# Gate and up as seven products of sums of quarters, and the whole modulation on TensorE

## The chip, the cores and the metric

The kernel runs on one core of one Trainium2 chip. The metric is the device time of one execution in microseconds. The kernel before takes 1740.79 us (median of 3 runs, 1739.17 to 1743.87).

## The reference

One step of a hybrid backbone on 640 token rows (512 latent tokens and 128 context tokens) of width 1024, two layers deep. Everything is float32.

```python
def trunk_layer(x, mod, s0, prm, l, pool_seg):
    sh1, sc1, g1, sh2, sc2, g2 = jnp.split(mod, N_MOD, axis=-1)
    h = rmsnorm(x, prm['norm1_g'][l]) * (1 + sc1) + sh1
    cols = jnp.einsum('bnd,de->bne', h, prm['w_in'][l])          # 1024 -> 2832 columns
    ...                                       # delta rule, spatial gating, pooling -> ya, yb, yc
    mix = jnp.einsum('bne,ed->bnd', jnp.concatenate([ya, yb, yc], axis=-1), prm['w_out'][l])
    x = x + g1 * mix
    h = rmsnorm(x, prm['norm2_g'][l]) * (1 + sc2) + sh2
    gate, up = jnp.split(jnp.einsum('bnd,df->bnf', h, prm['w_gu'][l]), 2, axis=-1)   # FF = 2816 each
    x = x + g2 * jnp.einsum('bnf,fd->bnd', jax.nn.silu(gate) * up, prm['w_down'][l])
    return x, s_fin
# mod = silu(c) @ w_mod[l] + b_mod[l]: 6 x 1024 numbers for each of two conditionings (latent, context)
```

## The kernel before, in words

Activations lie transposed: a tile holds 128 features on its rows and the 640 tokens as columns, in two halves of 320. Every large product is made three times to keep float32's accuracy: the weight block and the activations are each split into a rounded part and a rest (`wh`, `wl` and `xhi`, `xlo`, or `ah`, `al`), and `mm3` (L335) issues wh x hi, wh x lo and wl x hi as three matmuls of 128 x 128 weights on 320 columns. A weight block comes by a DMA on SyncE's queue (`wload`, L297) into one of two buffers; `wsplit` (L306) rounds it on ScalarE (L322) and takes the rest on VectorE (all but three of its 128-column blocks) and on GpSimd (the last three, L326).

A layer has three stages, and with the two layers they stand in this order: mix0, out0, ffn0, mix1, out1, ffn1.

- mix: the products with `w_in` (`gemm_xs`, L348), 22 blocks and the logits; the delta rule in chunks, and the two other branches. Many small matmuls and many steps on VectorE and ScalarE run among the large ones.
- out: the products with `w_out` (L1296), eight output blocks of 48 matmuls, each followed by the residual (`resid`, L448) and by the scaled and split operands of the next stage (`Norm.add`, L403).
- ffn: 22 units of 128 hidden columns. Each unit is two calls of `gemm_xs` (gate and up, 48 matmuls each: 8 blocks of k, 2 halves, 3 products). The norm isn't applied beforehand: the operand is x times (1 + scale), the shift rides along as two columns in front of the first half (322 columns), and each evacuation multiplies by the row statistics `rst` and adds the shift's part. After 8, 8 and 6 units the products with `w_down` follow (L1399). The last six units of layer 1 end the kernel with transposes, the final norm and the outputs.

The modulation needs 12,288 numbers per conditioning. Two sixths of layer 0 come first, as matmuls with 32 columns of weights, four row blocks side by side on four column strips of the array (`first_mod_`, L499). The other ten sixths are 160 steps of 512 columns x 128 rows (`pump_`, L257): VectorE multiplies and adds for one conditioning (L125), ScalarE multiplies for the other (L150) and GpSimd adds (L282); after eight steps `mod_sums` (L224) sums over the rows, by transposes on TensorE or by VectorE's own transpose and small matmuls. A table says how many steps follow each half of a product; they run from mix0 to the end of ffn0.

The program's instructions are ordered by a scheduler: each has a priority by its place in the program, moved by the offsets of `PRI` (L39), and each engine then takes its own in that order. PSUM has three buffers `acc`, three `dl` and two `md`.

Of the kernel before, what the change touches and what calls it, by code (L numbers as in the profile page):

```python
# [16 lines left out]
D = 1024  # L17
# [14 lines left out]
POUT = 1  # L32
# steps of the modulation after each half of a product, by branch
PUMPS = {'log0': (0, 0), 'k00': (0, 0), 'q00': (1, 2), 'sgu0': (1, 1), 'z0': (0, 1), 'v10': (1, 1), 'q10': (0, 0), 'v00': (1, 0), 'k10': (0, 1), 'pool0': (1, 0)}
# [11 lines left out]
def host_constants():  # L46
# [10 lines left out]
    # from here on: not kept on chip as they are  # L57
# [34 lines left out]
def tile_hybrid_step(ctx: ExitStack, tc: tile.TileContext,  # L92
# [59 lines left out]
    class at:  # L152
        """the instructions inside come that much earlier in the order of issue"""
# [11 lines left out]
    def behind(ins, prev):  # L165
        """queues one instruction of an engine behind another"""
# [10 lines left out]
    def in_turn(key, ins):  # L177
        """instructions of one kind in the order of the program"""
# [29 lines left out]
    quarters = const.tile([P, 32], F32, name="quarters")  # L208
    selr = const.tile([P, 15, P], F32R, name="selr")
# [9 lines left out]
    # steps: 512 columns x 128 rows of w_mod; a step's load is issued some steps ahead of its arithmetic  # L219
    SIXTHS = [(0, 2), (0, 4), (0, 3), (0, 5), (1, 1), (1, 0), (1, 2), (1, 4), (1, 3), (1, 5)]  # L220
    steps = [(l, w * D + c0, k) for l, w in SIXTHS for c0 in (0, 512) for k in range(KT)]
    ps_ = {"i": 0, "j": 0, "ma": None, "wm": {}, "due": None, "at": "mix0"}

    def mod_sums(l, c0, ma):  # L224
        t0 = c0 // P
        if ps_["at"] != "ffn0":
            for s in range(2):
                pt = md()
                for cb in range(4):
                    nc.tensor.transpose(pt[:, cb * P:(cb + 1) * P], ma[:, s, cb * P:(cb + 1) * P], ident)  # L230
                m = mod[:, l, s, t0:t0 + 4]
                nc.vector.tensor_reduce(m, pt.rearrange("p (c n) -> p c n", c=4), op=ADD, axis=AX.X)
                tt(m, m, bmod[:, l, t0:t0 + 4], ADD)
            mod_scales(l, c0)
            return
        # sums over the 32 rows of each quarter, then over the quarters
        ms = sm.tile([P, 2, 16], F32, tag="ms", name="ms", bufs=1)
        for s in range(2):
            pt = md()
            nc.vector.transpose(pt, ma[:, s])  # L240
            nc.vector.tensor_reduce(ms[:, s], pt.rearrange("p (c n) -> p c n", n=32), op=ADD, axis=AX.X)
        pt = md()
# [1194 lines left out]
```

## Time and profile before

| | |
|---|---|
| runs | 1740.79 us median, 1739.17 to 1743.87 |
| span of the profiled execution | 1737.7 us |
| PE busy | 1666.4 us (96%), 12952 matmuls |
| DVE, ACT, POOL busy | 1155.2 (66%), 761.1 (44%), 585.3 us (34%) |
| chain that ended last | PE 53%, of which the large products (`acc`) 47% |
| DMA | 174.34 MB, mean 100 GB/s |

The span is what the profile shows of one execution; the shortest run lies 1.5 us above it, the median 3.1 us. PE's mean duration of a matmul (316 ns) isn't its price: matmuls are pipelined, and from start to start there is less. A stretch's price is read from how many matmuls start in it. Idle time of an engine other than PE costs nothing unless PE waits for it.

### The profile page before, as it was taken

How to read it: one execution, taken by the hardware profiler on the slowest of the kernel's cores; microseconds unless marked ns; L12 is line 12 of the kernel's file. 1: busy time of each engine (PE TensorE's matmuls, PEld its weight loads, DVE VectorE, ACT ScalarE, POOL GpSimd, SP SyncE). 2: the span in 40 equal slices, each digit the busy share in tenths (PEclk: the TensorE clock that was granted, in tenths of full speed). 3: DMA queues.
4: the chain of work that ended last, by engine and by line, in shares of the span. 5: the costliest groups of instructions: out<-in, count | busy, mean ns of one | idle time of the engine just before them, and what ended most of it. 6: DMA issues, size and time to landing. Idle time of an engine off the chain costs nothing.

```text
span 1737.7 us, 33153 instructions
## 1 busy us (share of the span) xinstructions
PE 1666.4 (96%) x12952; PEld 1603.2 (92%) x12952; DVE 1155.2 (66%) x2462; ACT 761.1 (44%) x1564; POOL 585.3 (34%) x578
## 2 busy tenths in 40 slices
PE   6999999998899999999999999999999999999997
PEld 4788989988899999999998899999999999999997
DVE  6698688799888688877467777675544434433454
ACT  4557765554444344434246656543322212321232
POOL 3342330367645454554164112013411221222110
PEclk8999999999999999999999999999999999999999
DMA  9431231444444544453241211113222222222221
GB/s 316 143 98 57 68 99 29 150 127 139 145 141 141 154 137 143 143 158 103 62 144 52 62 38 50 37 51 126 83 73 74 79 79 74 74 73 73 74 85 61
DMA packets 243379, 174.34 MB, mean 100 GB/s; under 512 B 10006, under 2 KB 212376, under 8 KB 243224
## 3 DMA queue, kind: packets, MB, share of 16 engines
q1 hardware_dynamic: 231888, 157.44, 29.8%
q10 hardware_dynamic: 10184, 12.29, 2.2%
q0 software_dynamic: 1152, 2.51, 0.4%
q8 instruction: 102, 1.67, 0.4%
q14 instruction: 53, 0.43, 0.1%
HBM read 163.29 MB, written 8.91 MB: 99 GB/s over the span
## 4 chain that ended last, share of the span: by engine, by line
PE 53%; DVE 3%; ACT 1%; issue 1%; POOL 0%; DMA 0%; DVEq 0%; POOLq 0%; ACTq 0%
PE acc L117 47%; PE dl L117 5%; DVE wl L122 0%; PE md L117 0%; DMA w<-in_w_down_dram 0%; PE dl L1379 0%; DVE cv L125 0%; POOL guh L830 0%; PE md L760 0%; DVE yt L125 0%; DVE st L125 0%; DVE Z L122 0%; ACT wh L322 0%; ACT MT L945 0%; DVE SI L122 0%
## 5 line engine op out<-in xcount | busy, mean ns | idle before, releaser
L117 PE MATMUL acc<-xhi,wh 128*128 128x322 f32 (+2 forms) x2112 | 667.4, 316 | 5.4 <-DVE ga L122 4.6
L117 PE MATMUL acc<-xlo,wh 128*128 128x322 f32 (+2 forms) x2112 | 666.0, 316 | 1.4 <-DVE xlo L125 1.2
L117 PE MATMUL acc<-xhi,wl 128*128 128x320 f32 (+1 forms) x2080 | 655.0, 315 | 5.1 <-DVE wl L122 5.1
L326 POOL TENSOR_TENSOR wl<-w,wh 128x384 fp32r<-128x384 f32 x188 | 258.7, 1376 | 792.5 <-ACT wh L322 777.9
L117 PEld LDWEIGHTS acc<-xhi,wh 128*128 128x128 f32 (+1 forms) x2112 | 399.4, 189 | 10.7 <-PE acc L117 7.2
L117 PEld LDWEIGHTS acc<-xlo,wh 128*128 128x128 f32 (+1 forms) x2112 | 400.2, 189 | 4.1 <-POOL spp L1148 1.5
L117 PEld LDWEIGHTS acc<-xhi,wl 128*128 128x128 f32 x2080 | 396.4, 191 | 6.6 <-DVE wl L122 5.9
L322 ACT CAST wh<-w 128x1024 fp32r<-128x1024 f32 (+1 forms) x188 | 194.5, 1035 | 343.4 <-PE acc L117 282.6
L282 POOL TENSOR_TENSOR ma<-ma,wm 128x512 f32<-128x512 f32 x140 | 207.2, 1480 | 133.5 <-ACT wm L150 113.8
L122 DVE TENSOR_TENSOR wl<-w,wh 128x640 fp32r<-128x640 f32 (+1 forms) x188 | 213.3, 1134 | 50.5 <-ACT wh L322 23.9
L117 PE MATMUL acc<-ah,wh 128*128 128x320 f32 (+2 forms) x632 | 195.6, 309 | 0.7 <-ACT ah L1322 0.7
L117 PE MATMUL acc<-al,wh 128*128 128x320 f32 (+2 forms) x632 | 195.1, 309 | 0.1
L117 PE MATMUL acc<-ah,wl 128*128 128x320 f32 (+2 forms) x632 | 195.1, 309 | 0.0
L150 ACT ACTIVATE wm<-wm,sc 128x512 f32<-128x512 f32 x140 | 101.1, 723 | 135.0 <-DVE ma L125 117.8
L125 DVE SCALAR_TENSOR_TENSOR x<-acc,mod,x 128x128 f32<-128x128 f32 (+3 forms) x192 | 77.9, 434 | 119.8 <-PE acc L117 119.5
L125 DVE SCALAR_TENSOR_TENSOR ma<-wm,sc,ma 128x512 f32<-128x512 f32 x140 | 134.9, 964 | 25.6 <-DMA wm<-in_w_mod_dram 24.7
L117 PEld LDWEIGHTS acc<-ah,wh 128*128 128x128 f32 x632 | 118.7, 188 | 1.2 <-ACT ah L1322 1.1
L117 PEld LDWEIGHTS acc<-al,wh 128*128 128x128 f32 x632 | 118.7, 188 | 0.3 <-DVE al L122 0.3
L117 PEld LDWEIGHTS acc<-ah,wl 128*128 128x128 f32 x632 | 118.7, 188 | 0.0
L1322 ACT CAST ah<-ga 128x320 fp32r<-128x320 f32 x88 | 40.5, 460 | 155.9 <-DVE ga L125 155.9
L150 ACT ACTIVATE ga<-ga,bt 128x320 f32<-128x320 f32 x132 | 57.4, 468 | 89.9 <-DVE ga L122 89.9
L122 DVE TENSOR_TENSOR ga<-acc,rst 128x320 f32<-128x320 f32 x88 | 42.4, 483 | 73.9 <-PE acc L117 73.4
(369 smaller groups left out, 2481.7 us busy)
## 6 DMA issues: line engine op xcount, KB each, us to landing
w<-in_w_gu_dram SPq DMA_DIRECT2D x88, 512.0 KB, 3.7
wm<-in_w_mod_dram SPq DMA_DIRECT2D x162, 256.0 KB, 2.9
w<-in_w_in_dram SPq DMA_DIRECT2D x44, 512.0 KB, 3.6
w<-in_w_down_dram SPq DMA_DIRECT2D x32, 512.0 KB, 4.2
w<-in_w_out_dram SPq DMA_DIRECT2D x32, 256.0 KB, 3.0
wf<-in_w_mod_dram SPq DMA_DIRECT2D x30, 256.0 KB, 6.5
w<-in_w_down_dram SPq DMA_DIRECT2D x16, 384.0 KB, 3.4
x<-xd ACTq DMA_DIRECT2D x16, 320.0 KB, 4.7
```

Source lines behind the costliest of these rows:

```text
L117: return nc.tensor.matmul(o, lhsT=l, rhs=r, start=st, stop=sp, **kw).ins
L122: recent["v"] = nc.vector.tensor_tensor(o, a, b, op=op).ins
L125: recent["v"] = nc.vector.scalar_tensor_tensor(o, a, s, b, op0=op0, op1=op1).ins
L150: recent["a"] = nc.scalar.activation(o, i, f, **kw).ins
L282: nc.gpsimd.tensor_tensor(ma[:, 1], ma[:, 1], wm, op=ADD)
L322: nc.scalar.copy(wh, v)
L326: nc.gpsimd.tensor_tensor(wl[:, c:], v[:, c:], wh[:, c:], op=SUB)
L1322: nc.scalar.copy(hi[:, sl], ga[:, sl])
```

## The change

Four parts.

1. All but the first units of ffn (4 in layer 0, 3 in layer 1, made as before, gate and up together) are made by seven products in place of eight. With the k blocks and the tokens in halves, gate and up of one unit are a product of 2 x 2 quarters. `t_sums` makes four sums and differences of the quarters of h once per layer; each unit makes sums S1 to S4 of quarters of its weights and splits them as it splits weights (`Unit.prep`). A product is 4 blocks of k x 3 = 12 matmuls of 320 columns, so a unit has 84 in place of 96. Three intermediate sums are read out of one PSUM tile between the products that add into it (`Unit.go`: P6, P7 and P4 wait for the reading before them). `NEED` and the loop at the end say in which order a unit's products and the next unit's stand.
2. So that token quarters can be added, h is normalised, scaled and shifted before the products (`stats`, then h, hhi, hlo), in two parts of 384 and 256 tokens; there are no shift columns and no `rst` in ffn's evacuations any more. The last two blocks of out are reordered so that the first part of all blocks is done first.
3. The modulation's ten sixths are 40 groups of four matmuls side by side (32 x 512), a copy of 512 columns to SBUF and four matmuls with two columns. They stand in the mix stages alone, 0.6 groups after each half of a product in layer 0 and 0.45 in layer 1.
4. The pieces of ffn are 4, 4, 4, 5, 5 units instead of 8, 8, 6, and the products with `w_down` follow each. The selection matrices `selr` are made anew in each layer.

The diff's core (comments are also removed throughout):

```diff
+SHARE = (0.6, 0.45)
-W32, WM, WHL = 2, 3, 2
+W32, WM, WHL = 2, 4, 2
+PIECES, NPL = (4, 4, 4, 5, 5), (4, 3)
+NACT, NFT, NS = 5, 5, 3
+NEED = {"P2": ("g",), "P1": (), "P5": ("S1",), "P6": ("S2",), "P7": ("S3",), "P4": ("u2",), "P3": ("S4",)}
...
+    def mod_columns(ws, l, c0, k0, msb):
+        pm = md()
+        for i, w in enumerate(ws):
+            g = 32 * (i % 4)
+            mm(pm[g:g + 32, :], sc[:, k0 + i, :], w, i < 4, i >= len(ws) - 4, tile_position=(0, g))
+        copy("msb", msb, pm, "v")
+        pt = md()
+        for cb in range(4):
+            mm(pt[:, 2 * cb:2 * cb + 2], msb[:, cb * P:(cb + 1) * P], C("I16")[:, 0:2], True, True)
...
-                behind_recent("v", stt, ma[:, 0], wm, sc[:, k, 0:1], ma[:, 0], MUL, ADD)
-                behind_recent("a", times, f"pump{ps_['at']}", wm, wm, sc[:, k, 1:2], "a")
-                nc.gpsimd.tensor_tensor(ma[:, 1], ma[:, 1], wm, op=ADD)
...
+            def stats(q):
+                t0, t1, _ = PARTS[q]
...
+                for ch in range(c0, c1):
+                    mm(pc[:, ch:ch + 1], ss[:, ch * P:(ch + 1) * P], ones[:, 0:1], True, True)
+                ts(st[:, 1, c0:c1], pc[:, c0:c1], 1.0 / D, EPS, MUL, ADD)
+                rsqrt(st[:, 0, c0:c1], st[:, 1, c0:c1], st[:, 2, c0:c1])
...
+            for q in range(2):
...
+                for k in range(KT):
...
+                    tt(h[k][:, sl], x[k][:, sl], rsts[q][:, 0:t1 - t0], MUL)
+                    for a, b, s in segs:
+                        act(h[k][:, a:b], h[k][:, a:b], AF.Identity, scale=sc1[:, l, 1, s, k:k + 1],
+                            bias=mod[:, l, s, 24 + k:25 + k])
+                    nc.scalar.copy(hi[:, sl], h[k][:, sl])
+                    tt(lo[:, sl], h[k][:, sl], hi[:, sl], SUB)
...
+                def split(self, w):
+                    hi, lo = (self.W.tile([P, 4, P], F32R, tag=f"s{c}", name=f"s{c}", bufs=NS) for c in "hl")
+                    nc.scalar.copy(hi, w)
+                    tt(lo, w, hi, SUB)
...
+                    elif which == "P6":
+                        self.prod(self.o1, self.b2, Tb, g, False)
...
+                            self.gb_ = ft("gb")
+                            nc.scalar.copy(self.gb_, self.o1)
+                    elif which == "P7":
+                        self.prod(self.o1, self.b3, Ta, g, False)
...
+                            tt(self.ub, self.o1, self.ub, ADD)
+                    elif which == "P4":
+                        self.prod(self.o1, self.bu, Tb, f, False, True)
...
+                            tt(self.ga, self.o1, self.ga, MUL)
...
+                    unit_go(j, "P5")
+                    unit_go(j, "P6")
+                    if nx:
+                        unit_go(nx, "P2")
+                    unit_go(j, "P7")
+                    if nx:
+                        unit_go(nx, "P1")
+                    for w_ in ("P4", "P3") if nx else ("P3", "P4"):
+                        unit_go(j, w_)
```

How instructions move. TensorE in mix0, before: the modulation's only rows there are transposes (`ma`), four at a time, among the delta rule's (`SI`, `MT`) and the large ones.

```order
L806 MATMUL md<-r_ident,cv 128x128
L230 MATMUL md<-r_ident,ma 128x128 x4
L117 MATMUL acc<-xhi,wl 128x320
L117 MATMUL dl<-SI,MT 64x64
L117 MATMUL acc<-xhi,wh 128x320
L117 MATMUL acc<-xlo,wh 128x320
```

The same engine in mix0 now: one group's side-by-side matmuls (`md<-wm,sc`), and a group's four with two columns (`md<-cst,msb`).

```order
L120 MATMUL md<-cst,msb 128x2 x4
L120 MATMUL md<-wm,sc 32x512 x2
L120 MATMUL dl<-S_1051,selr 128x320 x3
L120 MATMUL md<-wm,sc 32x512
L120 MATMUL acc<-xhi,wl 128x322
L120 MATMUL acc<-xhi,wh 128x322
L120 MATMUL acc<-xlo,wh 128x322
L120 MATMUL dl<-S_1051,selr 128x320 x3
L120 MATMUL md<-wm,sc 32x512
```

This group's four matmuls have been parted by others into runs of 2, 1 and 1. Over the program 19 groups stand whole, and the 40 groups make 69 runs (51 in mix0, 18 in mix1).

TensorE where ffn1 begins, before: the last block of out is followed at once by the first products of gate, whose operand needs no statistics.

```order
L117 MATMUL acc<-mixqT_13819,wl 128x320
L117 MATMUL acc<-mixvn_13821,wh 128x320
L117 MATMUL acc<-mixvn_13822,wh 128x320
L117 MATMUL acc<-mixvn_13821,wl 128x320
L117 MATMUL acc<-xhi,wh 128x322
L117 MATMUL acc<-xlo,wh 128x322
```

The same place now: the statistics' matmuls (`ss`) stand between the last block of out (256 columns) and the first products with the normalised rows (`hhi`, `hlo`).

```order
L120 MATMUL acc<-mixqT_13962,wl 128x256
L120 MATMUL acc<-mixvn_13964,wh 128x256
L120 MATMUL acc<-mixvn_13965,wh 128x256
L120 MATMUL acc<-mixvn_13964,wl 128x256
L120 MATMUL dl<-ss,cst 128x384
L120 MATMUL md<-cst,ss 128x1 x2
L120 MATMUL acc<-hhi,wh 128x384 x2
L120 MATMUL acc<-hlo,wh 128x384
```

What comes behind them waits for the statistics, where it did not.

ScalarE in ffn1, before, over one unit: two roundings of weights (`wh`), the activations of gate and the roundings of the result (`ah`).

```order
L150 ACTIVATE ga<-ga,bt 128x320
L322 CAST wh<-w_15557 128x1024
L150 ACTIVATE ga<-ga,bt 128x192
L150 ACTIVATE ga<-ga,bt 128x128
L1322 CAST ah<-ga 128x320
L322 CAST wh<-w_15621 128x1024
L1322 CAST ah<-ga 128x320
```

The same engine in ffn1 now: `sh` are the roundings of weight sums, `ub`, `gb` and `ga` from `dl` or `acc` the readings of PSUM.

```order
L1410 CAST sh<-sv 128x512
L153 ACTIVATE gb<-gb 128x320
L1410 CAST sh<-wu 128x512
L1364 CAST ah<-ub 128x320
L1468 COPY ub<-dl 128x320
L1410 CAST sh<-sv 128x512
L304 CAST wh<-w_16031 128x1024
L1473 COPY gb<-acc 128x320
```

The reading `gb`, for which P7 waits, stands behind a rounding of sums and one of a whole weight block; 12 of the 37 units have these three in this order. The rounding ahead of it waits for P6 itself, since it writes into the buffer that P6 reads (three buffers, five splits per unit).

## Rows read from the trace of the kernel before

**Rows 1.** Windows by stage: duration, busy us of PE, PEld, DVE, ACT, POOL (x instructions), PEclk, DMA share, GB/s.

```profile
60.00:333.00 273.00, 260.99 (x2636) 246.01 (x2635) 223.60 (x592) 179.06 (x439) 88.60 (x107) 0.98 0.24 72
333.00:411.00 78.00, 69.67 (x430) 66.04 (x429) 66.86 (x91) 36.04 (x57) 46.85 (x37) 0.93 0.49 151
411.00:903.00 492.00, 479.33 (x3285) 471.95 (x3283) 381.65 (x604) 203.23 (x316) 252.71 (x194) 1.00 0.43 133
903.00:1184.00 281.00, 273.57 (x2741) 257.20 (x2740) 198.53 (x589) 162.42 (x404) 59.66 (x95) 1.00 0.19 54
1184.00:1246.90 62.90, 61.96 (x413) 59.79 (x412) 37.08 (x61) 24.41 (x39) 29.26 (x30) 1.00 0.36 112
1257.50:1669.00 411.50, 411.50 (x2783) 411.50 (x2783) 171.42 (x337) 105.74 (x165) 83.13 (x58) 1.00 0.25 74
```

**Rows 2.** Chain that ended last, ffn1: start us, us, what.

```profile
1257.48 411.65 PE acc L117 x2782
```

**Rows 3.** Timeline of PE: side-by-side matmuls, then matmuls of 20 columns: start us, us.

```profile
44.07 1.92 PE L117 MATMUL md<-wf,sc 128*32 128x512 f32 x16
45.93 0.41 PE L117 MATMUL dl<-xhi,eon 128*128 128x320 f32 x1
...
923.68 0.60 PE L117 MATMUL dl<-g,cst 128*128 128x20 f32 x4
924.12 0.38 PE L117 MATMUL dl<-g,r_V 128*128 128x20 f32 x2
```

**Rows 4.** Groups by form, the modulation's: busy us, mean ns, idle before.

```profile
L282 POOL TENSOR_TENSOR ma<-ma,wm 128x512 f32<-128x512 f32 x140 | 207.2, 1480 | 133.5 <-ACT wm L150 113.8 <-DVE ma L125 11.7 <-PE acc L117 2.0
L125 DVE SCALAR_TENSOR_TENSOR ma<-wm,sc,ma 128x512 f32<-128x512 f32 x140 | 134.9, 964 | 25.6 <-DMA wm<-in_w_mod_dram 24.7
L230 PE MATMUL md<-r_ident,ma 128*128 128x128 f32 x48 | 7.2, 286 | 2.7 <-POOL ma L282 1.6 <-DVE ma L125 1.2
L117 PE MATMUL md<-ms,quarters 128*32 128x8 f32 x112 | 3.5, 187 | 0.0
```

**Rows 5.** Waits of PE in out0 (333 to 411), then in ffn0's first part (425 to 545).

```profile
PE acc L117 <- DVE wl L122: 1.2, 1, 1.2
...
PE acc L117 <- DVE wl L122: 4.8, 2, 3.5
PE acc L117 <- DVE ga L122: 2.5, 4, 0.7
```

**Rows 6.** Groups by form in ffn1 (1260 to 1660).

```profile
L122 DVE TENSOR_TENSOR al<-ga,ah 128x320 fp32r<-128x320 f32 x40 | 20.2, 505 | 10.5 <-ACT ah L1322 10.5
L122 DVE TENSOR_TENSOR ga<-acc,rst 128x320 f32<-128x320 f32 x40 | 19.5, 487 | 59.6 <-PE acc L117 59.6
L322 ACT CAST wh<-w 128x1024 fp32r<-128x1024 f32 x56 | 58.8, 1050 | 176.1 <-PE acc L117 176.1
L1322 ACT CAST ah<-ga 128x320 fp32r<-128x320 f32 x41 | 18.9, 460 | 71.4 <-DVE ga L125 71.4
```

**Rows 7.** Tile `wl` in ffn1: duration ns min/median/max, first and last start.

```profile
L326 POOL TENSOR_TENSOR wl<-w,wh x56: 1054/1647/1656, 1265.3 to 1655.9; 128x384 fp32r<-128x384 f32 x56
L122 DVE TENSOR_TENSOR wl<-w,wh x56: 824/826/1643, 1265.4 to 1655.9; 128x640 fp32r<-128x640 f32 x56
```

**Rows 8.** Group by form in ffn0 (430 to 900).

```profile
L122 DVE TENSOR_TENSOR wl<-w,wh 128x640 fp32r<-128x640 f32 x57 | 76.3, 1338 | 18.9 <-issue 12.8 <-POOL ma L282 5.0 <-ACT wh L322 1.0
```

**Rows 9.** Timeline of DVE, the statistics of ffn1: first and last of the small steps.

```profile
1252.85 0.17 DVE L131 TENSOR_SCALAR st<-st 128x5 f32<-128x5 f32 x1
1255.05 0.17 DVE L125 SCALAR_TENSOR_TENSOR st<-st 128x5 f32<-128x5 f32 x1
```

**Rows 10.** Timeline of PE in out0, behind a wait.

```profile
402.24 0.41 PE L117 MATMUL acc<-mixMT,wl 128*128 128x320 f32 x1 [1.23 <-DVE wl L122]
404.28 0.47 PE L117 MATMUL acc<-mixZ,wh 128*128 128x320 f32 x1
405.61 0.47 PE L117 MATMUL acc<-mixSI,wl 128*128 128x320 f32 x1
```

**Rows 11.** Tile `msb`: the copy of a group's sums.

```profile
L147 DVE COPY msb<-md x2: 678/678/678, 22.0 to 32.7; 128x512 f32<-128x512 f32 x2
```

More of the change, by code (lines that the diff above doesn't have):

```diff
@@ L287, in pump_to, with mod_loads @@
-    def pump_to(l, w):
-        n = 2 * KT * (SIXTHS.index((l, w)) + 1)
-        while ps_["i"] < n:
-            pump()
-        if ps_["i"] == n and ps_["due"] is not None:
-            mod_sums(*ps_["due"])
-            ps_["due"] = None
+    def mod_loads():
+        while ps_["j"] < min(4 * len(groups), 4 * ps_["i"] + WM):
+            l, c0, k = groups[ps_["j"] // 4]
+            k += ps_["j"] % 4
+            wm = wp.tile([P, 512], F32, tag="wm", name="wm", bufs=WM)
+            nc.sync.dma_start(wm, w_mod[l, k * P:(k + 1) * P, c0:c0 + 512])
+            ps_["wm"].append(wm)
+            ps_["j"] += 1
@@ new lines, in pump_group, with pump @@
+    def pump_group():
+        with at("pump"):
+            i = ps_["i"]
+            l, c0, k0 = groups[i]
+            mod_loads()
+            ws = [ps_["wm"].pop(0) for _ in range(4)]
+            mod_columns(ws, l, c0, k0, sm.tile([P, 512], F32, tag="msb", name="msb", bufs=1))
+            if k0:
+                mod_scales(l, c0)
+            ps_["i"] += 1
+            mod_loads()
+    def pump(share):
+        ps_["sum"] += share
+        while ps_["sum"] >= 1.0 - 1e-6:
+            ps_["sum"] -= 1.0
+            if ps_["i"] < len(groups):
+                pump_group()
@@ L1296, in tile_hybrid_step @@
                 wb = wblock([(w_out[l, 4 * P:8 * P, cs], 0, 4), (w_out[l, 0:4 * P, cs], 4, 4)], 8, P)
-                gemm_act(wb, range(8), yb + ya, resid(l, 16, n, x[n]), POUT)
-                nrm.add(n, x[n], ft("sq"), shift=False)
-            pump_to(l, 3)
-            for n in range(KT):
-                nrm.shift(n)
-            rst = nrm.finish()
-            xs2 = nrm.xs
-            mark(f"ffn{l}")
-            ps_["at"] = f"ffn{l}"
-            pieces = (8, 8, 6)
-            f0 = 0
@@ new lines, in t_sums @@
+            def t_sums(k):
+                a, b = h[k], h[k + 4]
+                f, g = slice(0, HALF), slice(HALF, NT)
+                with at("tsums"):
+                    tt(a[:, f], a[:, g], a[:, f], SUB)
+                    tt(a[:, g], b[:, g], a[:, g], SUB)
+                    tt(b[:, g], b[:, g], a[:, f], SUB)
+                    tt(b[:, f], b[:, f], b[:, g], SUB)
+                    r = []
+                    for t, nm in ((a, "ta"), (b, "tb")):
+                        hi, lo = (tpool.tile([P, NT], F32R, name=f"{nm}{c}{k}") for c in "hl")
+                        nc.scalar.copy(hi, t)
+                        tt(lo, t, hi, SUB)
+                        r.append((hi, lo))
+                return r
@@ new lines, in pair, with acts_out, gu, unit_plain @@
+            def pair():
+                return tuple(acp.tile([P, NT], F32R, tag="ac", name=f"a{c}", bufs=2 * NACT) for c in "hl")
+            def acts_out(a, hi, lo, sl):
+                nc.scalar.copy(hi[:, sl], a)
+                tt(lo[:, sl], a, hi[:, sl], SUB)
+            def gu(j):
+                return [(w_gu[l, :, c:c + P], 0, KT) for c in (j * P, FF + j * P)]
+            def unit_plain(j):
+                hi, lo = pair()
+                wbs = [wblock([p_], KT, P) for p_ in gu(j)]
+                for q in range(2):
+                    t0, t1, _ = PARTS[q]
+                    sl = slice(t0, t1)
+                    os_ = [acc()[:, 0:t1 - t0] for _ in range(2)]
+                    first = last = None
+                    for k in range(KT):
+                        for o, wb in zip(os_, wbs):
+                            a, last = mmk(o, wb, k, hs[k], sl)
+                            first = first or a
+                    behind(first, recent.get("g"))
+                    recent["g"] = last
+                    with at("evac"):
+                        ga = xpool.tile([P, 384], F32, tag="sq", name="ga", bufs=2)[:, 0:t1 - t0]
+                        act(ga, os_[0], AF.Silu)
+                        tt(ga, os_[1], ga, MUL)
+                        acts_out(ga, hi, lo, sl)
+                return hi, lo
```

435 lines of the change are left out of this document (264 added, 171 removed).

## The prediction

> **What bounds the kernel now.** I read the windows by stage first. In ffn1 TensorE is busy for all of 411.5 us while VectorE has 171 and ScalarE 106 us of work [rows 1], and the chain that ended last runs through this stage as one piece of large products [rows 2]: there nothing but the number of matmuls sets the time. ffn0 makes the same products and carries most of the modulation: VectorE is busy 382 of 492 us and GpSimd 253 [rows 1]. Then I read who waited for whom: out0 and the start of ffn0 hold waits of TensorE for weight splits and evacuations on VectorE [rows 5]. In mix0 and mix1 TensorE is busy 261 of 273 and 274 of 281 us [rows 1], so what is put there is mostly paid.
>
> The price of a large matmul: 2782 start in 411.65 us [rows 2], 0.148 us each for 320 columns, of which 320 columns at 2.4 GHz are 0.133. The mean durations of the groups overlap and are no price.
>
> **Part 1, seven products.** 18 units in layer 0 and 19 in layer 1 have 84 matmuls in place of 96: 37 x 12 x 0.148 = **-65.7 us**, all on the path. The plain units' 384 + 256 columns cost what 2 x 320 do, and the products with `w_down` are as many as before; both count as nothing. Left are seven products of 1.78 us, 12.4 us per unit, and that is the time the other engines have.
>
> VectorE per unit: nine operations of 512 columns (four sums, five rests), the gate's rest of 640 and seven evacuations of 320. 320 columns cost 0.49 us [rows 6]. 640 cost 0.82 mostly and 1.64 at the worst [rows 7], and GpSimd is at the same split then. 512 lies at 0.70 by the columns between 0.505 and 0.826; by ffn0's mean of 1.34 for 640 [rows 8] it would be 1.07. I take 0.72, near the undisturbed row, since GpSimd now has one split of 1.65 us in 12.4. Sum: 9 x 0.72 + 1.1 + 7 x 0.49 = 11.0 us. ScalarE: 1.05 + 5 x 0.62 + 7 x 0.49 = 7.6 us (512 columns between 0.46 and 1.05, [rows 6]). Both fit, VectorE with a margin of a tenth.
>
> The waits inside: P7 adds into the tile that ScalarE must first have read after P6. With the next unit's P2 between, the cover is 1.78 us. In 12 units a rounding of sums (which itself waits for P6) and one of a weight block stand ahead of the reading: 0.2 (the matmul's end) + 0.62 + 1.05 + 0.46 + 0.1 = 2.4 us, 0.65 late, 12 x 0.65 = 7.8 us. In the others the weight block isn't behind it: 1.4 us, hidden. The last unit of a piece has no next unit: 0.2 + 0.46 + 0.1 = 0.75 us bare, in 4 + 5 pieces, 6.7 us. For the first unit of each piece, whose loads come behind those of `w_down`, I add 4 us as an estimate. Together **+18 us**, between 3 (ScalarE always early) and 60 (below).
>
> **Part 2, normalised rows.** Before, ffn1's first products need no statistics: from out's end at 1246.9 to 1669 [rows 1] it makes 2880 matmuls in 422 us, 0.147 each, and so loses nothing at its start. Now, after the last block's first part, there follow: residual, square, sum (0.55 each), small matmuls (0.4), eleven small steps at 0.20 (twelve from 1252.85 to 1255.05 and its end, [rows 9]) = 2.2, the diagonal (0.5), a matmul (0.5), then multiplication, shift and rounding of the first block (1.6); between them VectorE's queue has a weight split and the second part's residuals (1.8). That is 8.7 us and about 1.3 for ten handovers, 10 us, against 48 matmuls of 256 columns, 48 x 0.118 = 5.7 us (0.148 by the columns). 4 us are bare. Then VectorE makes a block of h in two operations of 0.55 with the second part's small steps between, 1.4 us per block, while TensorE uses one up in 6 x 0.175 = 1.05: 3 more. The second part has 16 shifts of 128 columns on ScalarE and as many VectorE operations, 9 us against 5.8: 3 more. **+10 us per layer, +20**; from 0 (all covered, as before) to 36 (VectorE at ffn0's rates). The sums of h (`t_sums`) lie beside the plain units, 14 us each, and cost nothing; without that cover they would cost some 10.
>
> **Part 3, the modulation.** Away go 140 + 20 steps on VectorE (0.96), ScalarE and GpSimd (1.48, [rows 4]). What TensorE gets back: out0 takes 78.0 us and out1, which has the same products and no modulation, 62.9 [rows 1]: **-15**. ffn0 takes 492.0 us [rows 1] against 3168 x 0.148 = 469: **-23** (its own transposes and small matmuls and the start's waits are in that).
>
> What TensorE must do instead: 16 side-by-side matmuls take 1.86 us to the next one's start, 0.465 per four [rows 3]. Side by side they share this time only if nothing stands between them; the 40 groups make 69 runs, and a run of one streams its 512 columns as long as four: 69 x 0.45 = 31 us. The 160 matmuls with two columns cost what four with 20 columns do, 0.44 us [rows 3]: 40 x 0.44 = 17.6. Together 48.7, 34.9 in mix0 and 13.8 in mix1. In mix0 some 40 of the 48 transposes go (7.2 us in all, [rows 4]), -5, and of the 12 us in which TensorE is idle there [rows 1] I let 5 be filled. **+25 in mix0, +14 in mix1**; from +15 (the runs fill idle time, or overlap with neighbours) to +49.
>
> **Part 4** moves matmuls from one piece to another: 0. `selr` anew is 15 small GpSimd copies where GpSimd is mostly free: 0.
>
> **Sum.** -65.7 + 18 + 20 - 15 - 23 + 25 + 14 = -27, from 1737.7 us of span to 1711; with the 3.1 us by which the median of the runs lies above the span, **1714 us**.
>
> **The rivals.**
>
> A, the waits are hidden: the readings come in time and the statistics lie under out's tail. For it: ffn1 before has no idle time at all with the same engines. Against it: the order of ScalarE's queue above, and a first product that can't start without statistics. -28 of the 38: 1686 us.
>
> B, VectorE becomes the bound of the units: if operations of 512 columns cost 1.07 us, a unit takes 9 x 1.07 + 1.34 + 7 x 0.55 = 14.8 us instead of 12.4: 37 x 2.4 = 89 in place of the 18, 1785 us, **slower**. The kernel is slower than before as soon as a unit takes (27 + 18) / 37 = 1.2 us more than 12.4, that is at about 0.96 us per operation. For it: ffn0 shows that rate [rows 8]. Against it: ffn0's GpSimd is busy half of the time, the units' a seventh.
>
> C, the mix stages choke on the groups' evacuation: there are two `md` buffers, shared with the delta rule's transposes, and one buffer for the copy. If each group holds TensorE for its copy of 0.68 us [rows 11], 40 x 0.7 = 28: 1742 us, no change. The Trainium skill has a rule for this (TensorEngine Tiling (Array Packing), PSUM Bottleneck): tiling speeds TensorE up but not the emptying of PSUM, which may then become the bottleneck. By that rule the groups would go at the copy's 0.68 us and not at 0.465; the trace has no stream of groups on which it shows. Against C: 27 groups in some 273 us are one in 10 us.
>
> D, the clock: behind a wait of 1.23 us in out0 matmuls started 0.27 us apart (404.28 to 405.61, five of them) instead of 0.148 [rows 10]: the granted clock fell to its lower level, 1.2 GHz, and was 0.93 over the stage [rows 1]. Such an episode of 4 us costs 1.9. At the two starts of ffn that is 4 us, inside my range; behind each of the 21 short waits too, 44 in all: 1758 us. Against it: ffn0 has waits of 0.6 us for `ga` [rows 5] and a granted clock of 1.00. The Trainium skill's rule (TensorE: Matmul & The Clock Gate, What's actually happening) is that the throttled state is the default and activity lifts it, so by it the starts of ffn are the places to look at; rows 10 agree that the clock falls behind a wait.
>
> **How the numbers follow.** Forecast 0.60, A 0.17, B 0.10, C 0.08, D 0.05. What a measurement can tell from no change is 0.3%, 5.2 us. Faster by more: nearly all of the forecast, A and a little of C, 0.78. Within: the rest of the forecast's spread and most of C, 0.08. Slower: B, D, and a tail of the forecast, 0.14. The forecast's own range is 1695 to 1733; to hold 8 in 10 it reaches to A and to C: **1680 to 1745**.
>
> **What would show it.** From the end of out1 to the end of the span it should be some 476 us, where before took 491 (1246.9 to 1737.7); the window should show TensorE idle at the start and about 1 us per piece for `gb`. mix0 should be 20 to 30 us longer, out0 about 15 shorter. Wrong would be: units of more than 13 us with VectorE busy throughout (B), waits for `msb` or `md` in mix0 (C), a granted clock below 0.97 in ffn (D), or no waits at all at ffn's start (A).

## The result, and the profile after

The changed kernel takes 1834.09 us (median, 1832.3 to 1836.15) where the kernel before takes 1739.98 (four runs now): a ratio of 1.054, 95% interval 1.0519 to 1.0562. It is slower by 94 us; the prediction was 1714, and its range ended at 1745.

The windows of the changed kernel by the same stages as [rows 1] (mix0, out0, ffn0, mix1, out1, and ffn1 to the end of the span):

```profile
60.00:410.80 350.80, 342.21 (x3070) 276.15 (x3069) 205.87 (x611) 156.19 (x407) 54.19 (x79) 1.00 0.37 115
410.80:483.00 72.20, 67.25 (x416) 62.81 (x414) 31.76 (x59) 19.52 (x33) 21.50 (x18) 0.93 0.28 88
483.00:954.00 471.00, 448.60 (x2949) 435.98 (x2948) 301.89 (x578) 197.06 (x368) 97.39 (x87) 0.99 0.26 78
954.00:1273.00 319.00, 309.23 (x2952) 274.00 (x2951) 210.73 (x619) 159.38 (x403) 65.43 (x108) 0.99 0.29 88
1273.00:1343.90 70.90, 67.46 (x417) 62.45 (x415) 31.97 (x60) 19.88 (x34) 20.90 (x18) 0.93 0.29 90
1343.90:1834.40 490.50, 457.24 (x2988) 442.47 (x2988) 311.15 (x620) 202.97 (x436) 76.59 (x62) 0.98 0.25 76
```

The kernel before, ffn1 to the end of the span:

```profile
1246.90:1737.70 490.80, 477.91 (x3218) 473.14 (x3216) 213.51 (x451) 133.45 (x271) 89.67 (x64) 0.99 0.25 74
```

| stage | before | after | difference | predicted |
|---|---|---|---|---|
| mix0 | 273 | 351 | +78 | +25 |
| out0 | 78 | 72 | -6 | -15 |
| ffn0 | 492 | 471 | -21 | -36 (-32 - 23 + 10 + 9) |
| mix1 | 281 | 319 | +38 | +14 |
| out1 | 63 | 71 | +8 | 0 |
| ffn1 to the end | 491 | 490.5 | 0 | -15 (-34 + 10 + 9) |

The windows begin at 60 us, whatever is done by then. The same matmul (`dl<-ss,cst`, 128 columns) begins at 50.0 us before and at 54.3 after, so 4 of mix0's 78 us are a later start. Most of the miss stands in mix0 and mix1, and TensorE is busy there (342 of 351 us): it isn't waiting, it has more to do than was priced. The rest is in out and ffn, where it has the fewer matmuls that were forecast and doesn't get done sooner.

First the mix stages. Timeline of TensorE in mix0 (start us, us, instruction, count):

```profile
202.48 1.05 PE L120 MATMUL md<-wm,sc 128*32 128x512 f32 x2
203.46 1.16 PE L120 MATMUL dl<-S,kT 128*128 128x128 f32 x8
204.54 1.06 PE L120 MATMUL md<-wm,sc 128*32 128x512 f32 x6
205.53 0.41 PE L120 MATMUL acc<-xhi,wh 128*128 128x322 f32 x1
205.79 0.31 PE L120 MATMUL acc<-xlo,wh 128*128 128x322 f32 x1
205.93 0.32 PE L120 MATMUL acc<-xhi,wl 128*128 128x322 f32 x1
...
209.05 0.95 PE L120 MATMUL md<-cst,msb 128*128 128x2 f32 x8
209.93 1.04 PE L120 MATMUL md<-wm,sc 128*32 128x512 f32 x2
210.90 0.49 PE L120 MATMUL dl<-R,kd 128*128 128x128 f32 x2
```

and the group of these matmuls in mix0 (busy us, mean ns):

```profile
L120 PE MATMUL md<-wm,sc 128*32 128x512 f32 x216 | 57.5, 610 | 2.5 <-DMA wm<-in_w_mod_dram 2.5
```

mix0 holds 27 groups of four, 108 matmuls, and the trace counts 216: a float32 matmul stands in the records as two instructions. So the run at 202.48 is one matmul, that at 204.54 three. One takes 0.98 us to the next start (203.46 - 202.48), three take 0.99 (205.53 - 204.54). Side by side does share the time, as predicted, but the time that is shared is 0.98 us and not 0.45. The four matmuls with two columns (x8) take 0.88, not 0.44. Added from start to start over all such rows: 54.0 and 22.7 us in mix0, 17.8 and 10.1 in mix1, 104.6 together, where 48.7 were predicted. The large product behind a run pays as well: the one at 205.53 takes 0.26 us to the next start, the one at 205.79 takes 0.14.

Then out1. Its first block is made for 384 tokens over all eight k, while the operands are still being made, and only then for 256 (idle time before an instruction, and who ended it, in brackets):

```profile
1287.84 0.69 PE L120 MATMUL acc<-mixvn,wh 128*128 128x384 f32 x1 [0.86 <-ACT mixvn L1067]
1288.70 0.69 PE L120 MATMUL acc<-mixvn,wh 128*128 128x384 f32 x1 [0.17 <-DVE mixvn L125]
...
1289.93 0.41 PE L120 MATMUL acc<-mixMT,wl 128*128 128x256 f32 x1
1290.14 0.63 PE L120 MATMUL acc<-mixQK,wh 128*128 128x256 f32 x2
...
1298.23 0.28 PE L120 MATMUL acc<-mixMT,wl 128*128 128x256 f32 x1
1298.35 0.40 PE L120 MATMUL acc<-mixQK,wh 128*128 128x256 f32 x2
```

At 1290 a matmul of 256 columns takes 0.21 us to the next start, at 1298 0.12: behind the waits the granted clock was at the lower of its levels, 1.2 GHz, as in [rows 10]. The window there shows it (0.50 of 2.4 GHz):

```profile
1284.00:1292.00 8.00, 6.80 (x24) 5.32 (x24) 3.58 (x7) 1.98 (x3) 0.00 (x0) 0.50 0.45 133
```

out1's mean is 0.93, where [rows 1] have 1.00.

ffn's waits are the expected ones, and more (waits of TensorE over the whole span: us, times, longest):

```profile
PE acc L120 <- ACT gb L1473: 21.3, 30, 1.2
...
PE acc L120 <- ACT wh L304: 4.5, 7, 0.7
PE acc L120 <- DVE x L128: 3.8, 6, 1.4
```

### The profile page after: what moved, and what is told of

It reads as the page before. It is cut to its first block, busy times and chain, and to the rows that moved or that the text cites. A ratio compares the mean times of both kernels' runs of the same rounds, so it can differ in the third digit from the quotient of the medians.

```text
span 1834.4 us, 33377 instructions
## 1 busy us (share of the span) xinstructions
PE 1733.4 (94%) x13014; PEld 1582.1 (86%) x13014; DVE 1125.6 (61%) x2612; ACT 775.8 (42%) x1715; POOL 357.9 (20%) x424
## 3 DMA queue, kind: packets, MB, share of 16 engines
q1 hardware_dynamic: 232400, 157.45, 28.1%
## 4 chain that ended last, share of the span: by engine, by line
PE 67%; DVE 9%; DMA 6%; ACT 4%; issue 3%; POOL 1%; SPq 0%; ACTq 0%; DVEq 0%; POOLq 0%
PE acc L120 48%; PE dl L120 12%; PE md L120 5%; DMA w<-in_w_gu_dram 2%; DMA wu<-in_w_gu_dram 2%; DVE sv L125 1%; DVE wl L125 1%; DVE sl L125 1%; DMA w<-in_w_down_dram 1%; ACT wh L304 1%; DMA wm<-in_w_mod_dram 1%; ACT sh L1410 1%; POOL wl L308 1%; DVE h L125 1%; ACT gb L1473 1%
## 5 line engine op out<-in xcount | busy, mean ns | idle before, releaser
L304 ACT CAST wh<-w 128x1024 fp32r<-128x1024 f32 (+2 forms) x183 | 162.4, 890 | 381.0 <-PE acc L120 291.7
L120 PE MATMUL acc<-xhi,wh 128*128 128x322 f32 (+3 forms) x704 | 229.5, 326 | 0.8 <-DVE wh L125 0.8
L120 PE MATMUL acc<-xlo,wh 128*128 128x322 f32 (+3 forms) x704 | 228.5, 325 | 1.1 <-DVE xlo L128 1.1
L120 PE MATMUL acc<-xhi,wl 128*128 128x320 f32 (+1 forms) x672 | 218.1, 325 | 0.0
L120 PE MATMUL acc<-hhi,wh 128*128 128x320 f32 (+2 forms) x520 | 166.3, 323 | 9.0 <-ACT wh L304 4.3
L120 PE MATMUL acc<-hlo,wh 128*128 128x320 f32 (+2 forms) x520 | 166.6, 320 | 2.2 <-DVE hlo L125 1.7
L120 PE MATMUL acc<-hhi,wl 128*128 128x320 f32 (+2 forms) x520 | 164.6, 318 | 2.8 <-DVE wl L125 2.6
L120 PEld LDWEIGHTS acc<-xhi,wh 128*128 128x128 f32 (+1 forms) x704 | 133.2, 189 | 22.6 <-issue 16.9
L120 PEld LDWEIGHTS acc<-xlo,wh 128*128 128x128 f32 (+1 forms) x704 | 132.6, 188 | 9.0 <-issue 5.7
L120 PEld LDWEIGHTS acc<-xhi,wl 128*128 128x128 f32 x672 | 128.6, 191 | 11.1 <-issue 10.1
L125 DVE TENSOR_TENSOR sl<-sv,sh 128x512 fp32r<-128x512 f32 x148 | 115.1, 777 | 14.2 <-ACT sh L1410 11.0
L120 PEld LDWEIGHTS acc<-hhi,wh 128*128 128x128 f32 x520 | 100.7, 194 | 14.2 <-ACT wh L304 5.5
```

The source lines that it names most:

```text
L120: return nc.tensor.matmul(o, lhsT=l, rhs=r, start=st, stop=sp, **kw).ins
L125: recent["v"] = nc.vector.tensor_tensor(o, a, b, op=op).ins
L304: nc.scalar.copy(wh, v)
```

## The experiments

Times are medians; ratios are to the kernel before on the same chip.

**The modulation taken out of both kernels.** no_mod, the changed kernel without the ten sixths:

```diff
-            mod_columns(ws, l, c0, k0, sm.tile([P, 512], F32, tag="msb", name="msb", bufs=1))
...
+                nc.vector.tensor_copy(mod[:, l, :, c0 // P:c0 // P + 4], bmod[...])   # k0 == 4
```

> The changed kernel without the modulation's ten sixths: their loads, their side-by-side matmuls, the copies and the matmuls with two columns are left out, and the bias alone stands for them. Theory P (price): in the changed kernel's trace the stretches that start with these matmuls add up to 104.6 us of TensorE (54.0 + 22.7 in mix0, 17.8 + 10.1 in mix1), and all of it is on the path: 1834 - 105 = 1729 us (1720 to 1736), mix0 (60 to 411) some 77 us shorter. Theory W (waits): only part of it is paid, since in mix0 TensorE had 12 us idle before and the delta rule's chains fill in behind; the rest of mix0's 78 us is order and waits that stay: 1770 to 1790 us.

1714.54 us, ratio 0.9847 (0.9822 to 0.9873): 120 us less, even more than theory P had. mix0 goes from 351 to 261.5 us, mix1 from 319 to 282. 15 us more than the 104.6 go: the same large matmuls and the delta rule's take 9 us less in mix0 (165.8 and 95.6 us from start to start, in place of 170.4 and 100.1, both from the matmul `dl<-ss,cst` on) and 6 in mix1. The trace shows where: in the changed kernel's mix0 a large product takes 0.25 us to the next start directly behind a run and 0.24 directly ahead of one, and 0.149 among its own kind. Theory W falls.

before_no_mod, the kernel before without its steps:

```diff
-                behind_recent("v", stt, ma[:, 0], wm, sc[:, k, 0:1], ma[:, 0], MUL, ADD)
-                ...
+                nc.vector.tensor_copy(mod[:, l, :, c0 // P:c0 // P + 4], bmod[...])   # k == 7
```

> The kernel before without the modulation's ten sixths (loads, steps on VectorE, ScalarE and GpSimd, sums and transposes are left out, the bias alone stands for them): the other half of the pair with no_mod, so that the difference of the two is what normalised rows, seven products and the new order of out bring by themselves. Theory G (the products gain what the prediction gave them, -65.7 + 18 + 20 = -28): 1714.5 + 28 = 1742 us, which would mean that the old modulation cost the kernel before nothing. Theory H (the old modulation cost out0 15 and ffn0 23 and some 10 in mix0, as the prediction's part 3 had it): 1740 - 48 = 1692 us, and then the products and the rows bring nothing, or cost 20.

1687.21 us, ratio 0.9689 (0.9675 to 0.9704); windows of its out0 and ffn0:

```profile
317.80:380.30 62.50, 61.57 (x411) 59.53 (x410) 36.73 (x60) 23.98 (x40) 28.48 (x29) 1.00 0.36 110
380.30:850.00 469.70, 468.97 (x3167) 467.73 (x3166) 208.52 (x414) 129.11 (x204) 110.51 (x88) 1.00 0.26 78
```

Theory H holds: out0 is 15.5 and ffn0 22.3 us shorter, as the prediction had it, and mix0 15. With no_mod this splits the result in two. The modulation costs 54 us in the kernel before and 120 in the changed one: +66. All the rest of the change, where -28 was forecast, costs 1714.5 - 1687.2 = **+27**.

**The price of a run.** whole_runs keeps a group's four together:

```diff
-        for i, w in enumerate(ws):
+        tc.cur_priority -= 4000
+        for i in [3, 0, 1, 2]:      # the one loaded last goes first
...
+        tc.cur_priority += 4000
```

> The changed kernel with the four side-by-side matmuls of each group kept together: the one whose weights are loaded last is issued first, and the four come ahead of other work once they are ready. By the order of instructions there are 41 runs in place of 70. Theory P: a run takes 0.98 us whatever its length (in the trace runs of 2, 4 and 6 instructions took the same), so 29 x 0.96 = 28 us go: 1806 us (1800 to 1812). Theory L (by length): the matmuls are paid one by one, and parting costs nothing: 1834. Theory W: the group now waits for its last load, at 1 us a time in 40 groups: 1820 to 1850.

1821.42 us, ratio 1.0461 (1.0438 to 1.0483): 13 less, not 28. In mix0 27 runs now take 27.7 us, most of them 1.00, so the price is theory P's, and L falls. But part comes back as theory W's waits:

```profile
PE md L120 <- DMA wm<-in_w_mod_dram: 8.2, 12, 2.0
```

groups_of_eight adds two groups into one PSUM tile:

```diff
-                mm(pm[g:g + 32, :], sc[:, k0 + i, :], w, i < 4, i >= len(ws) - 4, ...)
+                mm(pm[32 * j:32 * j + 32, :], sc[:, 4 * q + j, :], ws[j], q == 0, q == 1, ...)   # q = 0, 1
```

> The changed kernel with 20 groups of eight row blocks in place of 40 of four: the second four matmuls of a group add into the same PSUM tile, so that 20 copies and 80 matmuls with two columns are left of 40 and 160; the four of a run are kept together as in whole_runs. Theory P: whole_runs (1821) less 80 x 0.21 = 17 us of small matmuls: 1804 us (1798 to 1812). Theory W (loads bind the runs, 8.2 us of waits in whole_runs grow when a group's second four follow the first at once): 1815 to 1830.

1807.53 us, ratio 1.039 (1.0367 to 1.0414): 14 less than whole_runs, near P's 17; the waits for `wm` in mix0 grew to 15.0 us.

**The old modulation beside the seven products.** old_modulation has before's steps after products P5, P6, P7 and P1 of a unit and elsewhere as before:

```diff
                 units[j].go(which)
+                if which in ("P5", "P6", "P7", "P1"):
+                    pump()
```

> The changed kernel with the modulation of the kernel before: 160 steps on VectorE, ScalarE and GpSimd after the halves of products in mix0, the parts of out0, the products of ffn0's units and of w_down; one md group less per group. Theory P: TensorE is rid of 104.6 us; the steps cost in out0 and ffn0 what they cost before, some 15 + 23, and 10 in mix0: 1714.5 + 48 = 1762 us (1745 to 1775). Theory B (VectorE now binds: ffn0's 306 us of 478 and 96 steps of 0.96 us, of which each can hold up a unit's evacuation): 1780 to 1800.

1837.77 us, ratio 1.0547 (1.0527 to 1.0567): worse than even theory B. Its ffn0, and who is waited for there:

```profile
420.70:986.00 565.30, 482.24 (x3059) 459.39 (x3059) 476.08 (x763) 266.22 (x477) 236.44 (x184) 0.93 0.39 115
```

```profile
PE acc L121 <- ACT gb L1513: 21.8, 14, 5.1
PE acc L121 <- ACT wh L339: 12.4, 6, 5.2
PE acc L121 <- DVE ub L126: 10.3, 4, 4.1
```

VectorE is busy 476 of 565 us, and single waits reach 5 us: with the steps at these places the units leave no room for what ffn0 carried before for 22 us. Other places weren't tried.

**ffn's units.** gb_first moves one reading ahead in ScalarE's queue:

```diff
-                        with at("evac"):
+                        with at("gb"):            # PRI["gb"] = 300
                             self.gb_ = ft("gb")
```

> The changed kernel with ScalarE's reading gb ahead of the roundings of sums and weights in its queue. Theory Q (queue): the 30 waits for gb, 21.3 us, come from what stands ahead of it; a wait of 0.75 us stays at the end of each of the nine pieces and 0.2 at others: some 13 to 18 us go, 1834 to 1818 us (1814 to 1824). Theory S (shift): the roundings that come later are waited for instead (sh, wh), and the time stays: 1834, waits for sh or wh in place of gb.

1821.12 us, ratio 1.0462 (1.0439 to 1.0485), 13 less; ffn0 is 6 and ffn1 9 us shorter. The waits for `gb` over the whole span:

```profile
PE acc L120 <- ACT gb L1473: 11.9, 17, 1.1
```

Theory Q: 9.4 us of waits go. Of the 17 that stay eight are of 0.89 to 1.05 us, a piece's last unit that has no next one to cover it (predicted 0.75), the others of 0.30 to 0.85. Waits for `wh` are 4.6 us as before, so S falls.

all_plain makes all units plainly:

```diff
-PIECES, NPL = (4, 4, 4, 5, 5), (4, 3)
+PIECES, NPL = (4, 4, 4, 5, 5), (22, 22)
```

> The changed kernel with all 22 units of a layer made plainly, gate and up together with 96 matmuls, and no sums of h; normalised rows, pieces and the modulation on TensorE stay. 37 units x 12 x 0.148 = 65.7 us of matmuls come back. Theory W (waits): by the traces the stretches of units hold 15 and 18 us beyond their matmuls where the kernel before holds 2 in ffn1; if these 30 us are the seven products' own, the time is 1834 + 66 - 30 = 1870 us (1862 to 1878). Theory F (full gain, the waits come from pieces and loads and stay): 1900. Theory N (nothing gained by the seven products): 1834.

1931.14 us, ratio 1.109 (1.1073 to 1.1106): none of the theories. The new plain unit is itself slow. Two starts of units in its ffn0:

```profile
710.59 0.44 PE L120 MATMUL acc<-hhi,wh 128*128 128x384 f32 x1 [0.71 <-ACT wh L304]
711.45 0.44 PE L120 MATMUL acc<-hhi,wl 128*128 128x384 f32 x1 [0.24 <-DVE wl L125]
...
726.70 0.44 PE L120 MATMUL acc<-hhi,wh 128*128 128x384 f32 x1 [0.72 <-ACT wh L304]
```

A unit comes every 16.1 us, and 96 matmuls are 14.2. So this run is no measure of the seven products; it found a cost of the seven plain units that the change has kept. plain_seq takes it away from all but the first of each layer:

```diff
+            def unit_seq(j):
...
+                for which, p_ in enumerate(gu(j)):       # gate's two parts, then up's
+                    wb = wblock([p_], KT, P)
+                    for q in range(2):
...
             def unit_plain(j):
+                if j:
+                    return unit_seq(j)
```

> The changed kernel with its plain units (but the first of a layer) made as in the kernel before: gate's two parts first, then up's, in place of gate and up together. Theory B (buffers of weights): gate and up together hold both buffers of split weights until the unit's last matmul, so the next unit's rounding starts only then: in all_plain a unit came every 16.1 us where 96 matmuls are 14.2, with waits for wh (0.71) and wl (0.25 + 0.23). In the changed kernel this stands 3 + 2 times before a plain unit and twice before the first unit of seven products: 7 x 1.5 to 1.9 = 10 to 13 us less, 1834 to 1822 us. Theory A (PSUM: three acc tiles for parts of two): 1834.

1827.86 us, ratio 1.0494 (1.0475 to 1.0512): 6 us less, half of what theory B gave (3 in ffn0, 4 in ffn1).

**The start of ffn and of out.** no_stats:

```diff
-                    tt(h[k][:, sl], x[k][:, sl], rsts[q][:, 0:t1 - t0], MUL)
+                    tt(h[k][:, sl], x[k][:, sl], x[k][:, sl], MUL)          # and no stats(0), stats(1)
```

> The changed kernel without ffn's row statistics: their sums over rows, the eleven small steps, the diagonals and their matmuls are left out, and h is x times x in place of x times the statistics, so that VectorE's work on h stays. Theory R (the statistics hold up the start of ffn): from out1's end to 1372 the trace holds 14.3 us beyond the matmuls, where the kernel before holds 2.7 from 1246.9 to 1270; of that some 8 us per layer go, and the lower clock behind the wait with it: 1834 - 16 = 1818 us (1814 to 1824). Theory H (VectorE and ScalarE making h, 1.4 us per block, set the pace): 1828 to 1834.

1826.09 us, ratio 1.0483 (1.0459 to 1.0507): 8 us less, with single runs from 1820.59 to 1830.69, and 4 to 5 less in each ffn of the run in the trace. It lies between the theories; the lower clock that theory R names is what the trace shows most. The first 28.1 us of ffn1, two rows of the changed kernel and one of no_stats:

```profile
1343.90:1372.00 28.10, 24.65 (x103) 20.88 (x104) 24.34 (x68) 22.13 (x49) 1.00 (x1) 0.76 0.13 38
1348.00:1354.00 6.00, 6.00 (x18) 5.48 (x19) 6.00 (x23) 5.31 (x10) 0.00 (x0) 0.50 0.30 87
1333.40:1361.50 28.10, 22.45 (x119) 20.08 (x120) 27.95 (x59) 25.00 (x53) 5.45 (x3) 0.94 0.15 42
```

TensorE is idle for 3.5 us of them in the changed kernel and for 5.7 in no_stats, where the first product waits 2.9 us for `hhi`. It still starts 103 matmuls in the one and 119 in the other. The statistics' own matmuls take 1.8 us of the difference. The rest goes with the granted clock, 0.76 and 0.94: behind the changed kernel's waits TensorE goes at 1.2 GHz (0.50) for the six microseconds of the second row. That is rival D's mechanism. At ffn0's start the clock is 0.88 and 0.94. How the loss divides between the statistics and the making of h, the run doesn't show.

out_both:

```diff
+                for i in range(8):
...
+                    for o, (t0, t1, _) in zip(os_, PARTS):      # first block: both parts, k by k
+                        a, b = mm3(o, wh[i], wl[i], hi[:, t0:t1], lo[:, t0:t1], i == 0, i == 7)
...
```

> The changed kernel with the first block of out in another order: both parts of the tokens, block of k by block of k, as before the change, in place of first 384 tokens over all eight blocks of k and then 256. Theory O (order): with one part alone each newly made operand (mixQK, mixZ, ..., mixvn) has half of the matmuls to cover the making of the next, and the clock falls behind these waits; the first block took 16.5 us in out1 (1277 to 1293.8) where 48 matmuls are 7 us, so with both parts together some 6 us per layer come back, 12 in all: 1822 us (1816 to 1828). Theory E (evacuation and making of the operands set the end, not the order): 1834, and the waits stand at other operands.

1827.32 us, ratio 1.0501 (1.0475 to 1.0527). The interval overlaps the changed kernel's; the stages show theory O at half its size: out0 72.1 to 68.5 and out1 70.3 to 67.1 us.

**Putting it together.** all_mended has whole runs placed behind a product's last matmul, groups of eight, and the mends of out, `gb` and the plain units:

```diff
+    behind(mm(pm[32 * j:32 * j + 32, :], sc[:, k0 + j, :], ws[j], k0 == 0, k0 == 4, ...), recent.get("g"))
```

> The changed kernel with four edits: the four side-by-side matmuls of a group kept together and placed behind the last product before them, so that the loads have time; two groups adding into one PSUM tile, so 20 copies and 80 small matmuls are left; out_both, gb_first and plain_seq. If the causes found so far are all there is and add: 1714.5 (no_mod) + 40 x 0.98 + 20 x 0.85 = 56 for the modulation, less 7 (out_both), 13 (gb_first) and 10 (plain_seq): 1740 us (1735 to 1755). If the waits for loads stay as in groups_of_eight (18 us): 1760 to 1770.

1776.02 us, ratio 1.019 (1.0175 to 1.0206). 58 us of the 94 come back. The sum of the causes had given 1740 and the second figure 1760 to 1770; both were too low. out and ffn are now 1084 us in all (76.6 + 460.5 + 68.6 + 478.0), 1086 in before_no_mod, so they are even, though out0 is longer than in out_both (68.5), with one wait of 2.7 us for `mixvn`. The mix stages are 94 us longer than there, with 57.8 us of groups from start to start and 11.6 us of waits for `wm` in mix0. The rest is slower neighbours, other waits and a later start (`dl<-ss,cst` begins at 50.5 us there and at 55.1 here).

before_with_groups puts six groups of eight into the kernel before:

```diff
-    steps = [(l, w * D + c0, k) for l, w in SIXTHS for c0 in (0, 512) for k in range(KT)]
+    NPRE = 3
+    quads = [(l, w * D + c0, k0) for l, w in SIXTHS[:NPRE] for c0 in (0, 512) for k0 in (0, 4)]
...
+    steps = [(l, w * D + c0, k) for l, w in SIXTHS[NPRE:] for c0 in (0, 512) for k in range(KT)]
```

> The kernel before, with the first three of the ten sixths of the modulation (48 steps of VectorE, ScalarE and GpSimd, 32 in mix0 and 16 in out0) made as six groups of eight row blocks on TensorE in mix0, whole runs of four; the other 112 steps stay in ffn0. Theory P: the 32 steps cost mix0 15.3 us and the 16 cost out0 15.2 (before against before_no_mod), the groups cost 6 x (2 x 0.98 + 0.85) = 17: 1740.5 - 30.5 + 17 = 1727 us (1722 to 1733). Theory W (runs wait for loads, 1 to 2 us each, and md buffers are short): 1735 to 1745.

1744.41 us, ratio 1.0015 (1.0006 to 1.0023). Its mix0 and out0:

```profile
60.00:354.20 294.20, 283.66 (x2793) 252.93 (x2792) 194.81 (x568) 159.01 (x410) 52.09 (x88) 0.99 0.30 89
354.20:416.70 62.50, 61.56 (x411) 59.55 (x410) 36.75 (x60) 23.98 (x40) 28.57 (x29) 1.00 0.35 111
```

out0 gets its 15 us back, but mix0 is 36 us longer than without modulation (257.8), for groups that take 19.0 from start to start. Six of the 36 are a later start, since the window begins at 60 us: the same matmul without modulation, and here:

```profile
50.50 0.49 PE L117 MATMUL dl<-ss,cst 128*128 128x128 f32 x2
56.45 0.49 PE L117 MATMUL dl<-ss,cst 128*128 128x128 f32 x2
```

Counted from it on, the other matmuls, as many in both, take 7.5 us more, and idle time is 3.9 us more. So twelve visits of TensorE to another kind of work cost more than half as much again as the work, about 1 us around each visit. Why that much, and why the start is later, the runs don't settle; waits for `wm` are not among the longer waits here.

layer1_only and layer1_unchained leave layer 0 and the modulation as before and change out1 and ffn1 alone, mended; the second lets out's second block into the waits of the first:

```diff
+        if l == 1:
+            ...          # out1 and ffn1 of the changed kernel, with out_both, gb_first, plain_seq
-                        if i == 0:
+                        if i == 0 and (n, q) != (1, 0):      # layer1_unchained
                             behind(a, recent.get("g"))
```

> The kernel before in layer 0 and in both mix stages, with its own modulation; only out1 and ffn1 are those of the changed kernel, mended by out_both, gb_first and plain_seq (and selr made in each layer, for room). Theory L (the seven products pay by themselves where no modulation is): by all_mended out1 takes 68.4 us in place of 62.2 and ffn1 to the end 478.3 in place of 491.0: 1741 - 12.7 + 6.2 = 1734.5 us (1730 to 1739). Theory N (what the products save is lost whole in their waits and in the start, whatever the modulation): 1739 to 1745.

> layer1_only with one tie less: the second block of out, first part, need not come behind the whole first block, so that a third PSUM tile's matmuls can lie in the waits for newly made operands, as in the kernel before. Theory O (the order of out1's first blocks is what is left of out's loss: 68.4 against 62.2): layer1_only less 3 to 5 us: 1730 us (1726 to 1735). Theory E (it is the last blocks in two parts and the statistics' matmuls): as layer1_only.

1740.77 us, ratio 0.9988 (0.9978 to 0.9997), and 1736.84 us, ratio 0.9965 (0.9952 to 0.9977). out1 and ffn1 of the two:

```profile
1185.30:1253.60 68.30, 64.35 (x416) 60.46 (x414) 32.36 (x59) 19.50 (x34) 20.97 (x18) 0.98 0.30 93
1253.60:1737.10 483.50, 454.35 (x2988) 442.43 (x2988) 306.11 (x620) 202.88 (x436) 78.87 (x62) 0.98 0.26 77
```

```profile
1187.70:1252.00 64.30, 61.74 (x416) 58.59 (x414) 32.62 (x59) 19.34 (x34) 21.19 (x18) 1.00 0.32 99
1252.00:1736.10 484.10, 454.71 (x2989) 442.36 (x2988) 306.47 (x620) 202.75 (x436) 78.34 (x62) 0.98 0.26 77
```

ffn1 gains 7 us of its 34: TensorE's busy time falls by 23 us, from 477.9 to 454.7, and its idle time in the stage grows from 13 to 29. out1's loss of 5.4 falls to 1.4 with the tie gone, with a granted clock of 1.00: theory O. The second of them is the fastest kernel here that leaves no work out, 0.35% below the kernel before.

## Why the prediction was wrong, by its steps

- **Part 1, the matmuls: right.** TensorE's instructions in ffn1 to the end are 3218 before and 2988 now, 230 fewer; 19 x 12 = 228 were forecast.
- **The waits in the units: right in kind, short in size.** 21.3 us in 30 waits for `gb` where 14.5 in 21 were counted. VectorE's operation of 512 columns took 0.777 us (148 of them, `sl`), near the 0.72 taken; rival B doesn't hold, VectorE is busy 302 of ffn0's 471 us.
- **"The plain units ... count as nothing": wrong.** 6 us (plain_seq), and in all_plain each unit waits for `wh` and `wl`, as it would where gate and up together hold both weight buffers.
- **Part 2, the rows: right in size (+10 per layer), not in kind.** From out1's end to 1372 the trace holds 14.3 us beyond its matmuls, before 2.7 to 1270. The prediction made the whole of it of waits; only 3.5 us are idle time, and the granted clock of 0.76 over 28.1 us costs 0.24 x 28.1 = 6.7 us, an estimate. That the size came out near is luck to this extent.
- **The reordering of out was priced nowhere: a failed step.** out1 lost 8 us by it, and out0 got back 6 of its 15. The first block in both parts gives 3 to 4 of that in each layer (out_both), the tie to it another 4 in out1 (layer1_unchained), where 1.4 us stay lost.
- **Part 3, what TensorE gets back: right to a microsecond** (-15 and -23; before_no_mod has -15.5 and -22.3).
- **Part 3, what TensorE must do: the main failure.** [rows 3] show x16 in 1.86 us. I read this as 16 matmuls, four rounds of four; it is 8 matmuls in two instructions each, two rounds of 0.93. The same misreading halved the small matmuls. 69 runs x 0.98 + 40 x 0.84 = 101 us follow from the prediction's own formula with the right reading. The program's text would have told: one such block is eight matmuls. The Trainium skill would have, too (FP8 and Floating Point Precision, TensorE Precision Notes): true float32 takes four passes through the array. By it 512 columns are 4 x 0.237 us (0.148 by the columns) = 0.95 us, an estimate from the page and this case's price, and 0.45 could not be; the 0.98 measured agrees. The other 15 us, what a run costs its neighbours, were not in the sum at all.
- **Rivals C and D.** From 60 us on TensorE waits for no `msb` (the span's two waits, 7.0 us, lie ahead of it), so C falls. D is too large as a price behind every short wait: the mean clock is 0.99 in ffn0 and 0.98 in ffn1. But its mechanism is there, at out (0.93), where I did not look, and at the starts of ffn (0.88 and 0.76 over 28 us). D gave the two starts 4 us, and the sum had no term for them; by the clock they cost 3.4 and 6.7, estimates.
- **The range** allowed the modulation +49 at most, because both ends of that bound had been made with the same misread row.

The account: modulation +66 where the steps gave 48.7 - 10 - 15 - 23 = about 0; everything else +27 where they gave -28. The sum is 93, measured 94. no_mod against before_no_mod says where these 55 us lie: 17 in the two out stages (71.5 and 70.7 us against 62.5 and 62.6), 34 in the two ffn stages (473.0 and 493.8 against 469.7 and 490.7, where -28 was forecast), the rest in mix. The terms above make about half of ffn's 34. The other half, shorter waits (`x` 3.8 us, `ga` 2.9, `wl` 2.6) and slower matmuls behind them, no run takes apart, and none tries Part 4's pieces alone, which were priced at 0.

## What to carry to other kernels

Before a price is read from a row with a count, count the same instructions in the program: one operation can be two records, and a price then comes out at half. Work moved to the engine that bounds the kernel was paid in full here, with an extra for each change between kinds of work, so compare it with what it cost where it was: 54 us on engines with room against 120. A saving of matmuls by sums is worth only what its longer chains (sums, splits, readings between products, statistics first) leave of it; price the new order at every stage's start, where little work is ready to cover a wait, and price the lower clock behind the wait with it.

## What was not expected of the hardware

- A float32 matmul with 32 columns of weights and 512 moving columns takes 0.98 us alone, 0.99 with two others on the other column strips and 1.00 with three (whole_runs); the split operands' 320 columns take 0.148.
- A float32 matmul with two moving columns takes 0.21 us (four in 0.84), more than one of the split operands with 320 (0.148).
- Behind waits of only 0.17 to 0.86 us, one after every few matmuls in out1's first block, the matmuls went at the lower clock (granted clock 0.50 from 1284 to 1292 us), and still did three microseconds after the last of them at 1288.70.
- The clock lost at a start doesn't follow the idle time: over the first 28 us of ffn1 3.5 us of idle time go with a granted clock of 0.76, in no_stats 5.7 us with 0.94.
